# Eight raw buffers in turn for the expert weight blocks of a hybrid decoder step, three of them made of two half tiles from pools of the mixers

## Chip, cores and metric

One core of one Trainium2 chip runs one launch of the whole step. The metric is the device time of that launch in microseconds; less is better. The engines are named as in the profile: PE (TensorE, its weight loads PEld), ACT (ScalarE), DVE (VectorE), POOL (GpSimd) and SP (SyncE, which here only issues transfers).

## What is computed

The step runs two layers over 264 tokens (256 of a prompt, 8 decode tokens) of width 1024. Each layer mixes the tokens by three parallel groups (SSD, RWKV-7, GLA), projects, normalizes, and then has a channel mixer: a dense SwiGLU in layer 0, a top-2-of-8 mixture of experts in layer 1. The change touches the experts:

```python
def _moe(h, router, wg, wu, wd):
    logits = (h @ router).astype(jnp.float32)
    vals, idx = lax.top_k(logits, TOP_K)
    wts = jax.nn.softmax(vals, axis=-1)
    comb = jnp.sum(jax.nn.one_hot(idx, N_EXPERTS, dtype=jnp.float32) * wts[..., None], axis=-2).astype(h.dtype)
    out = jnp.zeros_like(h)
    for e in range(N_EXPERTS):
        out = out + comb[..., e:e + 1] * _swiglu(h, wg[e], wu[e], wd[e])
    return out
```

Each of `wg[e]`, `wu[e]`, `wd[e]` is 1024 x 1024 in f32.

## The kernel before

Every matrix product is made of three reduced-precision (fp32r) products: a weight block `w` is split into `wh`, its rounded copy, and `wl = w - wh`, and so are the activations; the product is xh·wh + xh·wl + xl·wh. A block is 128 x 1024 f32, 512 KB, and `block` (L380) does all of it: SP issues the transfer into a raw tile `w` (L384), ACT copies it to `wh` (through `act`, L296), DVE subtracts into `wl` (through `sub`, L317). The raw tile is free once both have read it; `wh` and `wl` are free once the block's last matmul has read them. `wh` and `wl` have three buffers each (`NW`, L253).

The experts' stage (`experts`, L1563) gathers each expert's tokens into 128 slots and runs the experts in four pairs. For one expert `up` (L1621) makes gate and up products in two halves of 512 columns, each half 2 x 4 blocks, then silu, product, four transposes and a split; `down` (L1644) makes the output in two halves of 4 blocks. That is 24 blocks an expert, 192 in all, used strictly in order. `expert_mm` (L1704) does a block: two k-slices, three matmuls of 512 columns each, in the order wh, wl, wh; so a block is six matmuls. After each block `pump` (L1613) may put in a step of gathering the next pair (tiles `xg`, `xo`, `sel`) or of scattering the previous one (`sc`).

Raw tiles come from two pools: `wts` (`self.wp`, three buffers, tag `w`) and `wada` (`self.ap`, two buffers, tag `wa`), the second otherwise used by the loads for the modulation (`ada`, L446, rows `wa<-in_wada`). The lambda `wl` at L1567 sends every block with an even number to `wada`, every odd one to `wts`:

```python
wl = lambda e, m, b: self.block(self.I["moe"][e, m, b], by="wmoe", spare=b % MOE["wa"] == 0)
```

Other tiles come from shared pools by a table (`T2`, L187): pool `g` has four buffers of 264 x 2 columns and serves, among others, `hk`, the four tiles that hold the experts' input; pool `m` has three and serves the decode states of the mixers (`srm` to `gsq`). `hk` is last read by the transposes `ht` (`rows`, L1517) at the head of the experts' stage.

Instructions are written in program order, and a scheduler orders them within each engine by priorities; tile reuse becomes semaphore waits. SP's queue runs in its order: a transfer that must wait for its buffer holds up all behind it. The last transfers before the stage are those of the output projection (`wout`, L637), the modulation (`wada`, L463) and the router (L1474).

Of the kernel before, what the change touches and what calls it, by code (L numbers as in the profile page):

```python
# [7 lines left out]
F32 = mybir.dt.float32  # L8
F32R = mybir.dt.float32r
# [157 lines left out]
def _unpack(r):  # L167
# [18 lines left out]

T2 = {'r': 'ai k r cs kk k2 ka rkt bk gn gr ah htl az',  # L187
 'd': 'hh hl cv qk gv zs xo bl xg al',
 'g': 'gqk gsc o hk sq rbt',
 'a': 'adae',  # L190
 'q': 'lw srw sss hts',
 'm': 'srm srv bx sst sgu sgl gsq'}
T1 = {'u': 'xt x ee fs raw', 'r': 'vt st vb q1 ab rt gt', 'd': 'xb', 't': 'w ends ed sm da dx rs8 mx cslot'}
TP = {'a': 'ada adat st',
 'd': 'pj op eg0 ed eg1 ssq pos lg',
# [3 lines left out]
ORDER = [['rwkv', 'conv', 'rstep', 'qkv', 'aff', 'sstep', 'rout', 'gstep', 'gla', 'ssd', 'z2', 'gread', 'z1', 'z0'],  # L199
 ['rstep', 'rwkv', 'conv', 'sstep', 'qkv', 'rout', 'gstep', 'aff', 'gla', 'ssd', 'z0', 'z1', 'z2', 'gread']]  # L200
X = {'FR': 1, 'AHEAD': 1, 'SA': 4}
MOE = {'s0': 28, 'ss': 6, 'g0': 31, 'gs': 5, 'wa': 2, 'e0': 11, 'es': 5}
LOW = {'rout.0': -9440,
 'win.1': -20,
 'sstep.0': -1560,
# [61 lines left out]
class Net:  # L267
    def __init__(self, nc, tc, I, O, stack):
        self.nc, self.tc, self.I, self.O = nc, tc, I, O
        p = lambda name, bufs, **k: stack.enter_context(tc.tile_pool(name=name, bufs=bufs, **k))  # L270
        self.cp = p("const", 1)
        self.wp = p("wts", NW["w"])
        self.ap = p("wada", NW["a"])
        self.hp = p("whi", NW["h"])
        self.lp = p("wlo", NW["l"])
        self.bp = p("big", 1)
        self.p2 = {t: p("f2" + t, n) for t, n in N2.items()}
        self.p1 = {t: p("f1" + t, n) for t, n in N1.items()}
        self.dp = p("scr", 1, space=bass.MemoryType.DRAM)
        self.pp = {t: p("ps" + t, n, space=PSUM) for t, n in NP.items()}  # L280
        self.late = None
        self.acts = []
        self.setname = None
        self.pre = None
        self.n = 0


    def act(self, out, in_, func=AF.Copy, bias=0.0, scale=1.0):
# [88 lines left out]
        return self.cst[:, o - 128:o - 128 + w]  # L377


    def block(self, src, n=1024, by="none", spare=False):  # L380

        self.n += 1
        w = (self.ap if spare else self.wp).tile([128, 1024], F32, tag="wa" if spare else "w", name=f"w_{self.n}")
        self.nc.sync.dma_start(w[:, :n], src)  # L384
        hi = self.hp.tile([128, 1024], F32R, tag="h", name=f"wh_{self.n}")
        lo = self.lp.tile([128, 1024], F32R, tag="l", name=f"wl_{self.n}")
        with self.low(by):
            self.act(hi[:, :n], w[:, :n])
            self.sub(lo[:, :n], w[:, :n], hi[:, :n].bitcast(F32))
        return hi[:, :n], lo[:, :n]  # L390
# [1172 lines left out]
    def experts(self, l, r, last, first=()):  # L1563

        nc, io = self.nc, self.C("iota")
        toks, mask, comb, pos, hth, htl = self.routed
        wl = lambda e, m, b: self.block(self.I["moe"][e, m, b], by="wmoe", spare=b % MOE["wa"] == 0)  # L1567
        if r:
            p = self.f1("posr", [128, 3, NE])
            self.ts(p, pos, -128.0 * r, OP.add)  # L1570
# [3 lines left out]
        def gather(pr):  # L1574

            sel = []
            for t, (t0, n) in enumerate(toks):
                s = self.f1("sel", [128, 2, 128], F32R)
                if t == 2:
                    nc.gpsimd.memset(s.bitcast(F32), 0.0)  # L1580
                for i in range(2):
                    e = 2 * pr + i
                    chosen = self.ts(s[:n, i], io[:n], pos[:n, t, e:e + 1], OP.is_equal, mask[:n, t, e:e + 1], OP.mult)
                sel.append(s)
            yield
            name = "xg" if pr % 2 else "xo"
            xg = [[self.f2(name, [128, 2, 256], F32R) for _ in range(4)] for _ in range(2)]
            for k in range(8):
                for x, src in zip(xg, (hth, htl)):
                    ps = self.ps("xg", [128, 256])  # L1590
                    for t, (t0, n) in enumerate(toks):
                        self.mm(ps, src[t, k // 4][:, k % 4], sel[t].rearrange("p a b -> p (a b)"), t == 0, t == 2)
                    done = self.act(x[k // 2][:, k % 2], ps)
                yield
            self.affine((chosen, done))
            pc = self.ps("cs", [128, 2])
            cslot = self.f1("cslot", [128, 2])
            selt = []
            for i in range(2):
                e = 2 * pr + i  # L1600
                for t, (t0, n) in enumerate(toks):
                    self.mm(pc[:, i:i + 1], sel[t][:n, i].bitcast(F32), comb[:n, t, e:e + 1], t == 0, t == 2)
                ps = self.ps("st")[:, :TT]
                for t, (t0, n) in enumerate(toks):
                    self.tr(ps[:, t0:t0 + n], sel[t][:n, i].bitcast(F32))
                s = self.f1("selt", [128, TT], F32R)
                self.act(s, ps)
                selt.append(s)
            self.act(cslot, pc)
            G[pr] = xg, selt, cslot  # L1610
            yield
# [43 lines left out]
        def scatter(pr):  # L1655
            selt = G[pr][1]
            if last and pr == 3:
                V["st"] = self.stats()
            st = V["st"]
            self.need(l, 5)  # L1660
            for d in range(8):
                ps = self.ps("sc")[:, :TT]
                todo = [(y[:, d % 4], selt[i]) for i, yh, yl in Y[pr, d // 4] for y in (yh, yl)]
                for j, (y, s) in enumerate(todo):
                    self.mm(ps, y, s, j == 0, j == 3)
                self.residual(l, 5, d, ps, st, last=st is not None)
                yield
# [8 lines left out]
        for pr in range(4):  # L1676
            ahead = gather(pr + 1) if pr < 3 else iter(())
            V["at"], V["side"] = 0, [(MOE["s0"], MOE["ss"], back), (MOE["g0"], MOE["gs"], ahead)]
            if pr < 3:
# [4 lines left out]
            else:  # L1684
                for i in range(2):
                    up(pr, i)
                for n in range(2):
                    for i in range(2):
                        down(pr, i, n)
                    if n == 0:  # L1690
                        for _ in back:
                            pass
                        back = scatter(pr)
                        V["side"] = [(V["at"] + MOE["e0"], MOE["es"], back)]
                break
# [8 lines left out]
    def expert_mm(self, ps, lhs, block, pump):  # L1704
        for q in range(4):
            hi, lo = block(q)
            for k in (2 * q, 2 * q + 1):
                xh, xl = lhs(k)
                w = slice(k % 2 * 512, k % 2 * 512 + 512)
                self.mm(ps, xh, hi[:, w], k == 0, False)  # L1710
                self.mm(ps, xh, lo[:, w], False, False)
                self.mm(ps, xl, hi[:, w], False, k == 7)
            pump()
# [25 lines left out]
```

## Time and profile before

| | us |
|---|---|
| median of 3 runs | 1132.21 |
| lowest and highest | 1125.35, 1136.5 |
| the profiled execution | 1124.54 |
| its span, first to last instruction | 1122.8 |
| PE busy in the span | 1023.5 (91%) |
| DVE busy | 741.4 (66%) |
| ACT busy | 609.1 (54%) |

The profile is of one execution, with a record of each instruction's start and duration and each transfer's landing. Matmuls are pipelined, so that PE counts as busy where they overlap; the step from one matmul's start to the next says more than its duration. Idle time is put down to what ended it. The mean granted TensorE clock was 0.96 of full speed, and 1.00 (2.4 GHz) throughout the experts' stage.

### The profile page before, as it was taken

The numbers are of one execution on the slowest core, as the hardware profiler recorded it, in microseconds if no ns is written. First come the engines' busy times: TensorE is split into PE (matmuls) and PEld (weight loads), VectorE is DVE, ScalarE is ACT, GpSimd is POOL, SyncE is SP. The second block draws the span as 40 slices with busy tenths as digits, with TensorE's granted clock in tenths as the row PEclk, the third lists the DMA queues.
The fourth block names the chain that finished last, engine by engine and source line by source line (L and its number), as shares of the span: only waits on it lengthen the run. The fifth ranks groups of instructions, "written<-read, shape, count | busy, mean of one in ns | idle before, by whom it ended". The sixth has DMA issues, their size and how long they took to land. (4 is left out here: it accounts for less than half of the span.)

```text
span 1122.8 us, 22443 instructions
## 1 busy us (share of the span) xinstructions
PE 1023.5 (91%) x8944; PEld 833.1 (74%) x8944; DVE 741.4 (66%) x1406; ACT 609.1 (54%) x1037; POOL 90.2 (8%) x191
## 2 busy tenths in 40 slices
PE   6889988789899999989899898979999999999994
PEld 2678766557799999978677775758777777778763
DVE  1577647654755545457786676476778888877884
ACT  2566323543554444348562445367767776776663
POOL 1031222000100000001411210010000000000000
PEclk9899989999899999999999989989999999999997
DMA  9774468754565555563863474316889988888881
GB/s 355 251 225 132 149 180 306 267 169 147 178 197 174 187 179 160 160 196 133 235 228 119 145 240 143 113 42 207 299 285 299 303 287 298 305 295 303 290 276 42
DMA packets 71184, 238.55 MB, mean 212 GB/s; under 512 B 9280, under 2 KB 10016, under 8 KB 71072
## 3 DMA queue, kind: packets, MB, share of 16 engines
q1 hardware_dynamic: 66512, 226.18, 61.1%
q0 software_dynamic: 4000, 10.71, 3.5%
q8 instruction: 72, 1.18, 0.4%
q14 instruction: 40, 0.33, 0.1%
q10 hardware_dynamic: 560, 0.15, 0.1%
HBM read 231.50 MB, written 5.51 MB: 211 GB/s over the span
## 5 line engine op out<-in xcount | busy, mean ns | idle before, releaser
L317 DVE TENSOR_TENSOR wl<-w,wh 128x1024 fp32r<-128x1024 f32 (+1 forms) x324 | 388.4, 1216 | 160.9 <-ACT wh L296 154.7
L296 ACT ACTIVATE wh<-w 128x1024 fp32r<-128x1024 f32 (+1 forms) x324 | 334.0, 1051 | 279.8 <-issue 79.5
L336 PE MATMUL pj<-hh,wh 128*128 128x264 f32 x384 | 122.1, 320 | 7.0 <-ACT cv L296 3.1
L336 PE MATMUL pj<-hl,wh 128*128 128x264 f32 x384 | 122.5, 320 | 0.4 <-DVE hl L317 0.4
L336 PE MATMUL pj<-hh,wl 128*128 128x264 f32 x384 | 120.6, 315 | 1.1 <-DVE wl L317 1.1
L336 PEld LDWEIGHTS pj<-hh,wh 128*128 128x128 f32 x384 | 80.0, 209 | 16.0 <-ACT hh L296 4.3
L336 PEld LDWEIGHTS pj<-hl,wh 128*128 128x128 f32 x384 | 79.7, 208 | 8.5 <-issue 6.0
L336 PEld LDWEIGHTS pj<-hh,wl 128*128 128x128 f32 x384 | 79.6, 208 | 7.6 <-issue 3.4
L336 PE MATMUL eg<-wh,xg 128*128 128x512 f32 x256 | 81.7, 397 | 0.5 <-ACT wh L296 0.5
L336 PE MATMUL eg<-wh,xo 128*128 128x512 f32 x256 | 81.7, 396 | 0.2 <-ACT wh L296 0.2
L336 PE MATMUL ada<-wa,sc 128*32 128x256 f32 x640 | 51.5, 404 | 27.0 <-DMA wa<-in_wada 23.2
L336 PE MATMUL ed<-wl,ath 128*128 128x512 f32 x128 | 52.9, 413 | 4.5 <-DVE wl L317 4.5
L336 PEld LDWEIGHTS eg<-wh,xg 128*128 128x128 f32 x256 | 48.1, 188 | 11.7 <-ACT wh L296 2.4
L336 PEld LDWEIGHTS eg<-wh,xo 128*128 128x128 f32 x256 | 48.1, 188 | 10.7 <-ACT wh L296 1.2
L336 PE MATMUL eg<-wl,xg 128*128 128x512 f32 x128 | 52.6, 411 | 3.8 <-DVE wl L317 3.6
L336 PE MATMUL eg<-wl,xo 128*128 128x512 f32 x128 | 52.6, 411 | 1.3 <-DVE wl L317 1.2
L336 PE MATMUL ed<-wh,ath 128*128 128x512 f32 x128 | 50.9, 397 | 0.4 <-ACT wh L296 0.3
L336 PE MATMUL fg<-hh,wh 128*128 128x264 f32 x176 | 50.8, 289 | 0.0
L336 PE MATMUL ed<-wh,atl 128*128 128x512 f32 x128 | 50.6, 395 | 0.0
L336 PE MATMUL fu<-hh,wh 128*128 128x264 f32 x176 | 50.5, 287 | 0.0
L336 PE MATMUL fu<-hh,wl 128*128 128x264 f32 x176 | 50.4, 286 | 0.0
L336 PE MATMUL fu<-hl,wh 128*128 128x264 f32 x176 | 50.4, 286 | 0.0
(486 smaller groups left out, 2288.7 us busy)
## 6 DMA issues: line engine op xcount, KB each, us to landing
w<-in_moe SPq DMA_DIRECT2D x192, 512.0 KB, 4.6
wa<-in_wada SPq DMA_DIRECT2D x80, 512.0 KB, 4.6
w<-in_win SPq DMA_DIRECT2D x48, 512.0 KB, 4.7
w<-in_ffgu SPq DMA_DIRECT2D x44, 512.0 KB, 3.7
k<-in_wada SPq DMA_DIRECT2D x32, 256.0 KB, 5.8
w<-in_wout SPq DMA_DIRECT2D x16, 512.0 KB, 4.9
w<-in_ffd SPq DMA_DIRECT2D x16, 512.0 KB, 3.5
w<-in_ffd SPq DMA_DIRECT2D x8, 384.0 KB, 3.9
```

The lines of the kernel that those rows point to most:

```text
L296: r = self.nc.scalar.activation(out, in_, func, bias=bias, scale=scale)
L317: return (e or self.nc.vector).tensor_tensor(out, a, b, op=op)
L336: return self.nc.tensor.matmul(out, lhsT, rhs, start=start, stop=stop)
```

## The change

The blocks of the experts' stage take their raw buffer from a string of eight letters in turn, `wawagwmg`: `w` is the pool `wts`, `a` is `wada`, `g` and `m` are two new names, `wg` and `wm`, in the mixers' pools `g` and `m`. A block of `g` or `m` is two tiles of 128 x 512 with a transfer, a conversion and a subtraction each. A counter runs over all blocks. No pool grows.

```diff
-  'g': 'gqk gsc o hk sq rbt',
+  'g': 'gqk gsc o hk sq rbt wg',
-  'm': 'srm srv bx sst sgu sgl gsq'}
+  'm': 'srm srv bx sst sgu sgl gsq wm'}
...
-MOE = {'s0': 28, 'ss': 6, 'g0': 31, 'gs': 5, 'wa': 2, 'e0': 11, 'es': 5}
+MOE = {'s0': 28, 'ss': 6, 'g0': 31, 'gs': 5, 'wa': 'wawagwmg', 'e0': 11, 'es': 5}
...
+        self.blocks = -1
...
-    def block(self, src, n=1024, by="none", spare=False):
+    def block(self, src, n=1024, by="none", home="w"):
 
         self.n += 1
+        if home not in "wa":
+            ws = [self.f2("wg" if home == "g" else "wm", [128, 512]) for _ in range(2)]
+            for i, w in enumerate(ws):
+                self.nc.sync.dma_start(w, src[:, i * 512:i * 512 + 512])
+            hi = self.hp.tile([128, 1024], F32R, tag="h", name=f"wh_{self.n}")
+            lo = self.lp.tile([128, 1024], F32R, tag="l", name=f"wl_{self.n}")
+            with self.low(by):
+                for i, w in enumerate(ws):
+                    cs = slice(i * 512, i * 512 + 512)
+                    self.act(hi[:, cs], w)
+                    self.sub(lo[:, cs], w, hi[:, cs].bitcast(F32))
+            return hi, lo
+        spare = home == "a"
...
-        wl = lambda e, m, b: self.block(self.I["moe"][e, m, b], by="wmoe", spare=b % MOE["wa"] == 0)
+        homes = MOE["wa"]
+
+        def wl(e, m, b):
+            self.blocks += 1
+            return self.block(self.I["moe"][e, m, b], by="wmoe", home=homes[self.blocks % len(homes)])
```

The order of instructions moves with it. The first number in a name counts the program's tiles. On SP, before, the queue ahead of the experts' stage is this; `w_1322` to `w_1325` are the expert blocks 0 to 3, `w_1327` to `w_1330` blocks 4 to 7, `w_1336` and `w_1337` blocks 8 and 9, and `w_1239`, `w_1243` the output projection's last two:

```order
L384 DMA w_1322_9294<-in_moe 128x1024
L384 DMA w_1324_9318<-in_moe 128x1024
L384 DMA w_1239_8911<-in_wout 128x1024
L384 DMA w_1243_8950<-in_wout 128x1024
L384 DMA w_1323_9306<-in_moe 128x1024
L384 DMA w_1325_9330<-in_moe 128x1024
L384 DMA w_1328_9355<-in_moe 128x1024
L384 DMA w_1327_9343<-in_moe 128x1024
L384 DMA w_1330_9379<-in_moe 128x1024
L384 DMA w_1329_9367<-in_moe 128x1024
L1474 DMA router_1256_9039<-in_router 128x256
L384 DMA w_1337_9417<-in_moe 128x1024
```

Of the change, the same place on SP, first part; `wm_1332` and `wm_1333` are the halves of block 6, `wm_1352` the first half of block 14, and blocks 0 to 3 have the names they had:

```order
L387 DMA wm_1332_9371<-in_moe 128x512
L387 DMA wm_1333_9372<-in_moe 128x512
L477 DMA wa_1235_8889<-in_wada 128x1024
L477 DMA wa_1236_8895<-in_wada 128x1024
L398 DMA w_1323_9306<-in_moe 128x1024
L398 DMA w_1325_9330<-in_moe 128x1024
L387 DMA wm_1352_9494<-in_moe 128x512
L398 DMA w_1239_8911<-in_wout 128x1024
L398 DMA w_1243_8950<-in_wout 128x1024
L398 DMA w_1322_9294<-in_moe 128x1024
L398 DMA w_1324_9318<-in_moe 128x1024
L398 DMA w_1330_9359<-in_moe 128x1024
```

Block 6 has moved ahead of two loads for the modulation, blocks 1 and 3 ahead of the output projection's last two, blocks 0 and 2 behind them; `w_1330` is now block 5. The queue goes on, around the router's load, with `w_1342` to `w_1344` blocks 8 to 10, `wg_1328` and `wg_1329` block 4, `wg_1335` and `wg_1336` block 7, `w_1345` block 11 and `wg_1348` block 12's first half:

```order
L398 DMA w_1342_9417<-in_moe 128x1024
L398 DMA w_1343_9429<-in_moe 128x1024
L398 DMA w_1344_9441<-in_moe 128x1024
L1488 DMA router_1256_9039<-in_router 128x256
L387 DMA wg_1328_9343<-in_moe 128x512
L387 DMA wg_1329_9344<-in_moe 128x512
L387 DMA wg_1335_9387<-in_moe 128x512
L387 DMA wg_1336_9388<-in_moe 128x512
L398 DMA w_1345_9453<-in_moe 128x1024
L387 DMA wg_1348_9466<-in_moe 128x512
```

Blocks 8 to 10 stand ahead of the router, where blocks 4 to 7 stood; blocks 4 and 7, in the tiles of `hk`, stand behind it. On DVE the subtractions at the head of the stage are these before, for blocks 3 to 8 (`w_1336` is block 8):

```order
L317 TENSOR_TENSOR wl_1325_9333<-w_1325_9330,wh_1325_9332 128x1024
L317 TENSOR_TENSOR wl_1327_9346<-w_1327_9343,wh_1327_9345 128x1024
L317 TENSOR_TENSOR wl_1328_9358<-w_1328_9355,wh_1328_9357 128x1024
L317 TENSOR_TENSOR wl_1329_9370<-w_1329_9367,wh_1329_9369 128x1024
L317 TENSOR_TENSOR wl_1330_9382<-w_1330_9379,wh_1330_9381 128x1024
L317 TENSOR_TENSOR wl_1336_9408<-w_1336_9405,wh_1336_9407 128x1024
```

and of the change, for blocks 3 to 6 and the first half of 7:

```order
L318 TENSOR_TENSOR wl_1325_9333<-w_1325_9330,wh_1325_9332 128x1024
L318 TENSOR_TENSOR wl_1329_9348<-wg_1328_9343,wh_1329_9347 128x512
L318 TENSOR_TENSOR wl_1329_9348<-wg_1329_9344,wh_1329_9347 128x512
L318 TENSOR_TENSOR wl_1330_9362<-w_1330_9359,wh_1330_9361 128x1024
L318 TENSOR_TENSOR wl_1333_9376<-wm_1332_9371,wh_1333_9375 128x512
L318 TENSOR_TENSOR wl_1333_9376<-wm_1333_9372,wh_1333_9375 128x512
L318 TENSOR_TENSOR wl_1336_9392<-wg_1335_9387,wh_1336_9391 128x512
```

The blocks keep their order on DVE (and on ACT); blocks of `g` and `m` have become two instructions of 512 columns.

## Rows read from the trace of the kernel before

**Rows 1.** Busy by stretch: start:end, length, PE, PEld, DVE, ACT, POOL, PEclk, DMA share, GB/s

```profile
14.00:28.00 14.00, 11.27 (x84) 4.61 (x84) 3.75 (x8) 4.45 (x7) 1.77 (x4) 1.00 1.05 400
28.00:42.00 14.00, 10.12 (x71) 7.23 (x72) 6.23 (x14) 6.36 (x10) 1.39 (x6) 0.88 0.78 284
...
678.00:708.00 30.00, 25.97 (x268) 19.50 (x270) 19.36 (x46) 14.38 (x34) 1.10 (x2) 0.94 0.35 125
...
765.00:1088.00 323.00, 312.36 (x1461) 247.89 (x1460) 259.34 (x313) 229.42 (x286) 0.62 (x2) 1.00 0.88 295
```

**Rows 2.** Waits, 760.6 to 1100.1 us: who waited for whom, us in total, times, longest

```profile
ACT wh L296 <- DMA w<-in_moe: 58.3, 63, 2.4
PEld eg L336 <- DVE wl L317: 11.5, 24, 1.1
PEld ed L336 <- DVE wl L317: 9.0, 17, 1.1
...
PEld eg L336 <- ACT wh L296: 3.6, 9, 0.7
...
PEld ed L336 <- ACT wh L296: 1.6, 3, 0.8
```

**Rows 3.** Timeline, one turn of a `wada` buffer: start, us, engine, instruction [idle before <-releaser]

```profile
795.23 0.33 SPq L384 DMA_DIRECT2D w<-in_moe  x1
...
799.62 1.06 ACT L296 ACTIVATE wh<-w 128x1024 fp32r<-128x1024 f32 x1 [0.80 <-DMA w<-in_moe]
...
800.71 1.23 DVE L317 TENSOR_TENSOR wl<-w,wh 128x1024 fp32r<-128x1024 f32 x1 [1.08 <-ACT wh L296]
...
801.97 0.33 SPq L384 DMA_DIRECT2D w<-in_moe  x1
```

**Rows 4.** The tensor `in_moe` after 765.2 us: its issues (duration ns, first, last), landing

```profile
L384 SPq DMA_DIRECT2D w<-in_moe x184: 327/328/792, 765.2 to 1088.6; - x184
...
DMA to landing us min/median/max: 3.6/4.7/6.8
```

**Rows 5.** Groups by form, 760 to 1100 us: count, busy us, mean ns, idle before <-releasers

```profile
L317 DVE TENSOR_TENSOR wl<-w,wh 128x1024 fp32r<-128x1024 f32 x189 | 225.5, 1222 | 65.1 <-ACT wh L296 60.1 <-PE eg L336 4.0 <-PE ed L336 0.5
L296 ACT ACTIVATE wh<-w 128x1024 fp32r<-128x1024 f32 x189 | 193.0, 1054 | 79.3 <-DMA w<-in_moe 58.3 <-DVE wl L317 6.8 <-DVE x L317 3.3
...
L336 PEld LDWEIGHTS eg<-wh,xg 128*128 128x128 f32 x256 | 48.1, 188 | 11.7 <-ACT wh L296 2.4
...
L317 DVE TENSOR_TENSOR atl<-eat,ath 128x512 fp32r<-128x512 f32 x16 | 10.9, 684 | 0.0
...
L296 ACT ACTIVATE ea<-eg 128x512 f32<-128x512 f32 x16 | 9.5, 594 | 3.6 <-PE eg L336 3.3
```

**Rows 6.** Timeline of PE, two expert matmuls that follow each other

```profile
886.44 0.40 PE L336 MATMUL ed<-wh,ath 128*128 128x512 f32 x1
886.67 0.40 PE L336 MATMUL ed<-wl,ath 128*128 128x512 f32 x1
```

**Rows 7.** Busy by stretch: from the first to past the last expert matmul

```profile
760.60:1100.10 339.50, 328.85 (x1546) 260.57 (x1546) 271.56 (x335) 241.60 (x306) 0.62 (x2) 1.00 0.85 285
```

**Rows 8.** The tile `sgl`: its readers `gso` on PE (duration ns, first and last start)

```profile
L336 PE MATMUL gso<-qk,sgl x64: 192/192/213, 683.7 to 685.4; 32*64 32x1 f32 x64
```

**Rows 9.** Timeline of SP and PE around the stage's start

```profile
687.62 0.33 SPq L463 DMA_DIRECT2D wa<-in_wada  x1
...
737.01 0.37 SPq L1474 DMA_DIRECT2D router<-in_router  x1
...
749.41 1.04 PE L369 MATMUL ht<-ident,hk 128*8 128x128 f32 x8
...
765.21 0.33 SPq L384 DMA_DIRECT2D w<-in_moe  x1
```

## The prediction

> **What bounds the kernel now.** I read the stretches first, then the waits, then single transfers. In the experts' stage (765 to 1088 us, 29% of the span) TensorE has work for 312.36 of 323 us at the full granted clock, and the transfer engines are busy 0.88 of the time at 295 GB/s [rows 1]: both look nearly full, so the shares alone decide nothing. The waits do. TensorE's weight loads stood 11.5 + 9.0 us for `wl` and 3.6 + 1.6 us for `wh`, 25.7 us at 24 + 17 + 9 + 3 = 53 places, and ScalarE, which makes `wh`, stood 58.3 us at 63 places for the landing of `w` [rows 2]. So TensorE waits for conversions, and these wait for transfers.
>
> Why are the transfers late, at 295 GB/s? The stretch 14 to 28 us moved 400 GB/s with the same 16 engines [rows 1]. They are late because they are asked for late. Even blocks live in the `wada` pool's two buffers, odd ones in `wts`'s three. An even block's transfer can't start before the even block four places earlier is converted. One turn of such a buffer can be read: the transfer was issued at 795.23; ScalarE started at 799.62, its 0.80 us of idle time ended by the landing; VectorE ran from 800.71 for 1.23 us; the next transfer was issued at 801.97 [rows 3]. That is 6.74 us for four blocks. From medians, a landing of 4.7 us, a conversion of 1.054 us, a subtraction of 1.222 us and some 0.1 us of hand-overs make 7.1 us, or 1.77 us a block [rows 3 to 5]. The stage's 184 transfers from 765.2 to 1088.6 us took 323.4 / 184 = 1.757 us each [rows 4]. The two-buffer loop explains the pace of the whole stage.
>
> What would TensorE do without it? Matmuls of 512 columns start 0.23 us apart [rows 6], six to a block, 192 blocks: 1152 x 0.232 = 267 us; the other matmuls fill the rest of the 339.5 us between 760.6 and 1100.1 [rows 7] that is not waiting, so the floor is 339.5 - 25.7 = 314 us, 1.63 us a block.
>
> **The change part by part.** *The ring.* Eight buffers in turn (3 `w`, 2 `wa`, 2 pairs `wg`, 1 and a half pairs `wm`) replace the split 2 + 3. Each block's transfer now waits for the block eight places earlier, so the 7.1 us loop spans eight blocks, 0.89 us a block, under TensorE's 1.63. What goes is the 25.7 us of waits. A little of it isn't loss: loads that follow each other without a wait also stand 0.232 - 0.188 = 0.044 us [rows 5], 53 x 0.044 = 2.3 us. Gain: 23.4 us.
>
> *What is late next.* `wh` and `wl` still have three buffers each. A conversion starts when TensorE leaves the block three places back and must be through before the second matmul of its own block: two blocks, 12 x 0.232 = 2.78 us, plus one matmul, 3.0 us in all; it needs 0.2 (ScalarE's start after a matmul, an estimate from the hand-overs in rows 3) + 1.05 + 0.03 + 1.22 + 0.05 = 2.55 us. The slack of some 0.45 us is eaten where ScalarE or VectorE has another operation of 0.59 to 0.75 us in front: the activation, transposed copy and output of each expert's half, 3 x 16 = 48 places. Each then costs about 0.68 - 0.45 = 0.23 us of TensorE, 11 us if all 48 meet a conversion and none if the transposes beside them give the time back. I take half, 6 us, and keep 0 and 12. For the low end speaks that 53 waits among 192 blocks are fewer than the 96 even ones: the odd blocks, whose data lie ready, go through the same ring of three today.
>
> *Halves.* Three of eight blocks, 72, are two transfers, two conversions and two subtractions of 512 columns. On VectorE 2 x 0.684 - 1.222 = 0.146 us more a block, 10.5 us; on ScalarE 2 x 0.594 - 1.054 = 0.134, 9.6 us [rows 5]. Both engines have room: VectorE's 271.56 us [rows 7] become 282 in some 322, 88%; ScalarE's 241.60 become 251, 78%. For such a block the first half is ready after 0.2 + 0.59 + 0.03 + 0.68 = 1.5 us rather than 2.55, so it has more slack, not less. Cost on the path: 0; if VectorE became the bound, up to 10.5 us, which the 12 us above already stand for. SP issues 264 transfers rather than 192, 0.33 us each [rows 3], 87 us of 320: no bound.
>
> *Ahead of the stage.* The new order puts the two halves of block 6 in front of two `wada` loads, the second half waiting for the mixers' last reader of its buffer. That reader, `gso` on TensorE, ends at 685.4 [rows 8]; the `wada` load behind it went out at 687.62 [rows 9]. Cover 2 us, cost 0; the transfer engines are busy 0.35 there [rows 1], so the extra 0.75 MB is carried for nothing. Blocks 8, 9 and 10 now stand ahead of the router's load, but they wait for the conversions of blocks 0, 1 and 2, the same three that blocks 4, 7 and 6 wait for now; the router still goes out at 737.0 [rows 9]. Blocks 4 and 7 use the tiles of `hk`, which are not dead yet: they wait for its last transposes, at 749.41 + 1.04 [rows 9], and everything behind them on SP waits too. Nothing there is wanted before 765: block 4 lands by about 755, and today SP stands from 737.0 to 765.21 anyway [rows 9]. When the stage starts, 11.5 blocks lie loaded instead of 8.
>
> *Sum.* The profiled execution took 1124.54 us (its span is 1122.8): 1124.5 - 23.4 + 6 = 1107.1 us. The median of the runs, 1132.21, is 7.7 us above it. A longer landing goes straight into the two-buffer loop: 0.1 us more is 46 turns x 0.1 = 4.6 us. If the runs differ by that, the change removes it; if by something else, it stays and the median is 1114.8. I take the middle, 1111 us.
>
> **One rule against the change.** The 256 KB halves fill the opening: 14 to 28 us, 400 GB/s [rows 1]. The Trainium skill (DMA: Bandwidth & Descriptors, Rules for kernel authors) wants transfers of 1 MiB or more for full bandwidth; by that rule cutting three of eight blocks in two is a step the wrong way, and the stage would stay bound by transfers. The trace disagrees as far as it goes: its best stretch is of halves. The sum keeps the row; the rule's case is the last rival.
>
> **The rivals.** *The conversions take over.* For: VectorE at 88% serves them in order, and the ring of three is short. Against: halves give slack, and odd blocks keep up today. At the 12 us bound and a bit more, 23.4 - 14 = 9 us are gained: 1115 on the profile's scale, 1119 to 1123 on the runs'. *The transfers are the bound already.* For: busy 0.88 at 295 GB/s. Against: the 400 GB/s, and SP waiting for buffers, not the engines. Then only the 3.5 blocks loaded ahead count, 3.5 x 1.757 = 6 us: 1118.5, or 1126 by the median. *No effect*, if `hk` or the order on SP held the prefetch so late that the early ring never fills: 1132. It would need SP to stand past 765, and what it waits for there is over at 750.5 [rows 9]. *Slower.* One mechanism: mixed whole and half transfers run less well than whole ones. After 765.2 180.5 blocks of 0.524 MB remain; under 180.5 x 0.524 / 323.4 = 292 GB/s the stage is longer than now. The stretch 28 to 42 us, a mix, shows 284 GB/s at a share of 0.78 [rows 1]; at that rate 180.5 x 1.846 = 333 us, 10 us more: 1134.5, or 1142 by the median.
>
> **How the numbers follow.** Forecast 0.74, with its own range 1100 to 1119; conversions 0.11; transfers 0.07; no effect 0.03; slower 0.05. 1% of 1132 is 11.3 us, about what a measurement of this kernel can tell from no change. The forecast gains 11 to 24 us and is faster by that but for its lowest part (0.03); of the conversions' case a third is. Faster 0.75, within 1% 0.21, slower 0.04 (the fifth of the slower case that stays within 1% goes there). The range 1100 to 1125 reaches through the conversions' case and leaves out the two beyond it and a little below.
>
> **What would show it.** Right: ScalarE's waits for the landing of expert blocks fall from 58.3 us to under 10, the weight loads' waits for `wl` from 20.5 us to about 6, and what is left is preceded by a late start of VectorE or ScalarE, not by a landing; transfers are issued 10 us or more before their conversion; the stage from the first to the last expert matmul is about 322 us. Wrong: conversions that still wait for landings at 300 GB/s (transfers), or VectorE busy throughout with TensorE waiting as long as before (conversions), or `wada`, `router` or `hk` reached later than 687.6, 737.0 and 750.5 us.

## The result, and the profile after

| | before | after |
|---|---|---|
| median of 4 runs of each, side by side on one chip | 1128.78 us | 1109.58 us |
| lowest and highest | 1123.45, 1136.5 | 1106.2, 1112.74 |
| the profiled execution | 1124.54 | 1112.09 |
| its span | 1122.8 | 1110.2 |
| first expert matmul starts at | 760.67 | 762.98 |
| the stage: to the end of the last expert matmul | 337.83 | 319.26 |
| the end: from there to the end of the span | 24.25 | 27.97 |

The ratio is 0.9856, with a 95% interval of 0.9809 to 0.9904: 11 to 22 us shorter. The last three rows of the table are read from the first and last record of the tiles `eg` and `ed` on TensorE; they add up to the span. The stage lost 18.6 us, the end gained 3.7, and the first expert matmul came 2.3 us later. Medians in this document are of all executions of a kernel, while ratios and intervals leave out the slow ones, more than 1.5% above that kernel's fastest.

Busy time by stretch of the kernel after, the four stretches of [rows 1] and one around the stage, as [rows 7] (start:end, length, PE, PEld, DVE, ACT, POOL, granted clock, DMA share, GB/s):

```profile
14.00:28.00 14.00, 11.39 (x84) 4.82 (x84) 3.75 (x7) 4.45 (x7) 1.77 (x4) 0.89 1.05 400
28.00:42.00 14.00, 10.32 (x68) 7.81 (x69) 6.62 (x15) 6.36 (x10) 1.39 (x6) 0.76 0.77 286
678.00:708.00 30.00, 26.05 (x258) 18.79 (x258) 18.51 (x45) 13.00 (x30) 1.10 (x2) 0.89 0.45 137
765.00:1088.00 323.00, 319.77 (x1536) 260.65 (x1534) 277.06 (x408) 250.83 (x374) 0.62 (x2) 1.00 0.83 294
762.90:1082.50 319.60, 316.37 (x1516) 259.42 (x1516) 274.10 (x394) 250.34 (x374) 0.62 (x2) 1.00 0.84 297
```

The reader is to see how little the shares tell: from 765 to 1088 us the transfer engines carry 294 GB/s, as before (295), at a lower share, and TensorE's busy time rises by 7 us. From 678 to 708 us the half transfers of blocks 6 and 14 in pool `m` are added (137 GB/s instead of 125).

The waits of the kernel after, 760.6 to 1100.1 us, against [rows 2] (who waited for whom, us, times, longest):

```profile
ACT wh L297 <- PE eg L337: 32.2, 99, 1.3
...
ACT wh L297 <- PE ed L337: 7.0, 22, 0.7
...
PEld ed L337 <- ACT ea L297: 2.0, 5, 0.5
...
PEld xg L337 <- ACT xg L297: 1.3, 4, 0.7
PEld xg L337 <- ACT xo L297: 1.1, 3, 0.7
...
PEld eg L337 <- DVE wl L318: 0.4, 2, 0.2
```

ScalarE's 58.3 us for landings are gone from the list. What it waits for now is TensorE, 39.2 us at 121 places, to free a buffer of the ring of three `wh`. Of the weight loads' 20.5 us for `wl`, 0.4 is left, in two waits. The line and the engine have turned round: conversions no longer make TensorE late, TensorE paces them. New in the list are waits of the weight loads for other results of ScalarE, the activation `ea` and the gathered inputs `xg` and `xo`, of which the list before has none.

The transfers after 765.2 us, against [rows 4], from the view of the tensor `in_moe`, and SP's queue in a piece of the stage:

```profile
L398 SPq DMA_DIRECT2D w<-in_moe x112: 327/328/755, 767.5 to 1066.6; - x112
...
DMA to landing us min/median/max: 3.2/5.0/7.3
```

```profile
816.42 1.04 SPq L387 DMA_DIRECT2D wg<-in_moe  x2
```

```profile
826.14 1.15 ACT L297 ACTIVATE wh<-wg 128x512 fp32r<-128x512 f32 x2 [0.28 <-PE ed L337]
```

The two transfers issued at 816.42 are converted at 826.14, 9.7 us later, and the 0.28 us of idle time ahead of that conversion is ended by TensorE, where [rows 3] had a landing. Over the records of the `wg` tiles issue and conversion lie 10.2 us apart (median), the landing 6.2 us before the conversion. A landing takes 5.0 us (whole and half transfers together) instead of 4.7, and ScalarE never waits for one.

### The profile page after: what moved, and what is told of

Read it like the earlier page. It is cut to its first block, busy times and chain, and to the rows that moved or that the text cites. A ratio compares the mean times of both kernels' runs of the same rounds, so it can differ in the third digit from the quotient of the medians.

```text
span 1110.2 us, 22791 instructions
## 1 busy us (share of the span) xinstructions
PE 1019.3 (92%) x8944; PEld 834.0 (75%) x8944; DVE 747.0 (67%) x1478; ACT 620.1 (56%) x1109; POOL 87.3 (8%) x191
## 5 line engine op out<-in xcount | busy, mean ns | idle before, releaser
L297 ACT ACTIVATE wh<-w 128x1024 fp32r<-128x1024 f32 (+1 forms) x252 | 264.8, 1052 | 222.4 <-issue 79.4
L318 DVE TENSOR_TENSOR wl<-w,wh 128x1024 fp32r<-128x1024 f32 (+1 forms) x252 | 304.7, 1215 | 124.5 <-ACT wh L297 121.4
L337 PE MATMUL pj<-hh,wl 128*128 128x264 f32 x384 | 118.1, 309 | 1.1 <-DVE wl L318 1.1
L337 PEld LDWEIGHTS pj<-hh,wh 128*128 128x128 f32 x384 | 77.3, 202 | 15.7 <-ACT hh L297 4.3
L337 PEld LDWEIGHTS pj<-hl,wh 128*128 128x128 f32 x384 | 77.0, 201 | 8.6 <-issue 6.2
L337 PEld LDWEIGHTS pj<-hh,wl 128*128 128x128 f32 x384 | 77.0, 201 | 8.0 <-issue 3.8
L318 DVE TENSOR_TENSOR wl<-wg,wh 128x512 fp32r<-128x512 f32 x96 | 61.9, 687 | 0.5
L297 ACT ACTIVATE wh<-wg 128x512 fp32r<-128x512 f32 x96 | 55.1, 623 | 6.6 <-PE eg L337 5.0
L337 PE MATMUL eg<-wl,xg 128*128 128x512 f32 x128 | 50.5, 395 | 0.0
L337 PE MATMUL fg<-hh,wl 128*128 128x264 f32 x176 | 50.5, 287 | 0.0
L337 PE MATMUL ed<-wl,ath 128*128 128x512 f32 x128 | 50.4, 394 | 0.0
```

What stands on the lines that cost most here:

```text
L297: r = self.nc.scalar.activation(out, in_, func, bias=bias, scale=scale)
L318: return (e or self.nc.vector).tensor_tensor(out, a, b, op=op)
L337: return self.nc.tensor.matmul(out, lhsT, rhs, start=start, stop=stop)
```

## The experiments

For every kernel the table gives the same readings of its profiled execution. The last two columns are a sum over the stage: for each matmul the time to the start of the next, less the median of its tile and shape, where that is over 20 ns; first where the next is an expert matmul (`eg`, `ed`), then where it is another one (gather `xg`, scatter `sc`, and the like). Each row is read from one trace.

| kernel | median us | first expert matmul | stage | end | stage + end | lost at `eg`, `ed` | at others |
|---|---|---|---|---|---|---|---|
| before | 1128.78 | 760.67 | 337.83 | 24.25 | 362.1 | 25.4 | 2.5 |
| after | 1109.58 | 762.98 | 319.26 | 27.97 | 347.2 | 5.7 | 5.6 |
| after, again | 1107.39 | 752.48 | 319.31 | 28.19 | 347.5 | 5.7 | 5.6 |
| turn `wawaw` | 1101.17 | 756.25 | 319.11 | 23.60 | 342.7 | 8.0 | 1.8 |
| turn `wawaw`, again | 1103.84 | 756.93 | 319.46 | 23.48 | 342.9 | 8.2 | 1.8 |
| turn `awagawam` | 1129.12 | 765.01 | 340.09 | 25.55 | 365.6 | 27.7 | 3.9 |
| turn `aaw` | 1209.91 | 757.16 | 426.39 | 24.25 | 450.6 | 99.6 | 13.6 |
| halves only, old turn | 1120.89 | 763.64 | 332.89 | 25.43 | 358.3 | 20.1 | 3.3 |
| all conversions in halves | 1112.10 | 767.55 | 320.00 | 27.86 | 347.9 | 3.9 | 8.0 |
| turn `wawawg` | 1108.19 | 758.11 | 317.15 | 27.68 | 344.8 | 6.1 | 3.1 |
| after, early scatter | 1107.57 | 770.54 | 323.07 | 24.82 | 347.9 | 6.3 | 5.9 |
| turn `wawaw`, early scatter | 1103.07 | 759.12 | 321.74 | 22.54 | 344.3 | 7.5 | 2.5 |

**A fair turn of the five old buffers.** The first question was whether the distance between two uses of a `wada` buffer set the pace (theory T1), or whether the room and the blocks loaded ahead did (T2).

```diff
-MOE = {'s0': 28, 'ss': 6, 'g0': 31, 'gs': 5, 'wa': 'wawagwmg', 'e0': 11, 'es': 5}
+MOE = {'s0': 28, 'ss': 6, 'g0': 31, 'gs': 5, 'wa': 'wawaw', 'e0': 11, 'es': 5}
```

> Only the five buffers of before (3 w, 2 wada), but in the fair turn w a w a w: no tile of the mixers, no halves, every transfer waits for the block five places earlier instead of four (wada) or six (wts). Theory T1, the distance of four set the pace: the 7.1 us loop spans five blocks, 1.42 us a block, under TensorE's 1.66 (319.3 us / 192 in the changed kernel); a landing of 6.8 us, the 90th percentile before, makes the loop 9.2 us or 1.84 a block, so some landings are still waited for. Stage from the first to the last expert matmul 322 to 328 us, ScalarE's waits for expert blocks under 20 us, time 1110 to 1118 us. Rival T2, more room and more blocks loaded ahead bring the gain: with five buffers the stage stays near 338 us and the time at 1125 to 1132 us.

1101.17 us (1100.29 to 1102.01), ratio 0.9766 to before (0.9721 to 0.9810). T1 holds, and T2 falls: without one tile of the mixers and without a half, the stage is as short as that of the changed kernel. Stage and time are even below what T1 expected. It had taken 6.8 us for the 90th percentile of the landings before; that is the longest of [rows 4], and the 90th percentile in the trace is 5.3 us, with which the loop over five blocks stays under TensorE's 1.66. The waits, 740 to 1110 us:

```profile
ACT wh L297 <- DMA w<-in_moe: 11.3, 22, 1.2
...
PEld eg L337 <- DVE wl L318: 3.7, 10, 1.1
PEld ed L337 <- DVE wl L318: 2.4, 6, 0.7
```

Five buffers are just enough: 50 of the 192 blocks landed less than 0.2 us before their conversion starts (the median is 0.6 us), and 22 are waited for, 40 in the second trace of this kernel. The changed kernel, with 6.2 us of margin at its `wg` blocks, loses 2.3 us less at the expert matmuls (5.7 instead of 8.0).

**Eight buffers, the even blocks still at four.**

```diff
-MOE = {'s0': 28, 'ss': 6, 'g0': 31, 'gs': 5, 'wa': 'wawagwmg', 'e0': 11, 'es': 5}
+MOE = {'s0': 28, 'ss': 6, 'g0': 31, 'gs': 5, 'wa': 'awagawam', 'e0': 11, 'es': 5}
```

> All eight buffers, but the turn is a w a g a w a m: the even blocks stay in the two wada buffers at a distance of four blocks as before, the odd ones go through w, g, w, m. T1: the loop of four blocks is still 7.1 us, so the pace stays at 1.75 us a block, the stage at 334 to 340 us and the time at 1124 to 1132 us, though six tiles' worth of room is added. T2: room and prefetch count, the stage is near 320 us and the time 1108 to 1114 us.

1129.12 us, ratio 1.0017 (0.9986 to 1.0047): no gain from three more buffers, and a stage of 340.09 us, at the top of what T1 expected. Its waits in the stage are those of [rows 2] again:

```profile
ACT wh L297 <- DMA w<-in_moe: 51.0, 56, 2.5
PEld eg L337 <- DVE wl L318: 13.2, 24, 1.1
PEld eg L337 <- ACT wh L297: 7.9, 17, 1.0
PEld ed L337 <- DVE wl L318: 6.9, 14, 1.1
```

The `wg` blocks of this kernel lay loaded for 22 us (median) before they were converted, but TensorE takes the blocks in order, and the `wada` block beside them was late.

**A distance of three.**

```diff
-MOE = {'s0': 28, 'ss': 6, 'g0': 31, 'gs': 5, 'wa': 'wawagwmg', 'e0': 11, 'es': 5}
+MOE = {'s0': 28, 'ss': 6, 'g0': 31, 'gs': 5, 'wa': 'aaw', 'e0': 11, 'es': 5}
```

> The five buffers of before in the turn a a w: a wada buffer comes back after three blocks. T1: 7.1 us / 3 = 2.37 us a block at the landing of before (4.7 us), 2.0 at the shortest tenth of landings (3.6 us); 192 blocks make a stage of 384 to 455 us and a time of 1175 to 1246 us; ScalarE waits for two of three landings. T2 (the number of buffers decides, whatever the turn): as with five buffers in the other turn.

1209.91 us, ratio 1.0729 (1.0668 to 1.0790): five buffers in another turn are far slower, as T1 said, and T2 falls again. The stage of 426.39 us is 2.22 us a block, times three a loop of 6.66 us. Before, 337.83 / 192 x 4 = 7.04; in the kernel `awagawam` 340.09 / 192 x 4 = 7.09. The loop is the same within the landing time, which is 4.4 us here and 4.7 there:

```profile
L398 SPq DMA_DIRECT2D w<-in_moe x181: 327/328/604, 768.0 to 1172.7; - x181
...
  ACT wh L297: 126.9, 92
...
DMA to landing us min/median/max: 3.4/4.4/5.8
```

ScalarE waits for 92 landings, not for two of three (128). (The 3.6 us that the expectation calls the shortest tenth is the shortest landing of [rows 4]; a tenth is under 4.2 us.)

With a distance of five the same loop would allow 1.4 us a block, and TensorE, which takes 1.66, sets the pace. That is the law of this stage in the turns measured: the pace is the larger of TensorE's time for a block and the loop over the distance.

**Halves alone.** The buffers and turn of before, every conversion in halves.

```diff
-            self.act(hi[:, :n], w[:, :n])
-            self.sub(lo[:, :n], w[:, :n], hi[:, :n].bitcast(F32))
+            for cs in ((slice(0, 512), slice(512, 1024)) if by == "wmoe" else (slice(0, n),)):
+                self.act(hi[:, cs], w[:, cs])
+                self.sub(lo[:, cs], w[:, cs], hi[:, cs].bitcast(F32))
...
-MOE = {'s0': 28, 'ss': 6, 'g0': 31, 'gs': 5, 'wa': 'wawagwmg', 'e0': 11, 'es': 5}
+MOE = {'s0': 28, 'ss': 6, 'g0': 31, 'gs': 5, 'wa': 'aw', 'e0': 11, 'es': 5}
```

> The buffers and the turn of before (even blocks in wada, odd in wts, distances four and six), and only the conversions of every expert block cut into halves of 512 columns; transfers whole. T1: the loop of a wada buffer becomes landing 4.65 + start 0.1 + ScalarE's half 0.61 + 0.05 + VectorE's two halves 2 x 0.687 + issue 0.1 = 6.9 us instead of 7.1 (the second half of ScalarE runs beside VectorE), 1.72 us a block: stage 328 to 336 us, time 1116 to 1126 us. Rival T3, the shorter chain from landing to the first matmul (about 1 us less for a first half) is what helped the changed kernel: the stage is near 320 us and the time near 1108 us.

1120.89 us, ratio 0.998 (0.9946 to 1.0014). The stage is 332.89 us, 6.94 us for four blocks against 6.9 reckoned: only what the halves cut from the loop is won. Landings are still waited for, here from 740 to 1110 us:

```profile
ACT wh L297 <- DMA w<-in_moe: 45.0, 48, 2.0
PEld eg L337 <- ACT wh L297: 9.4, 18, 1.1
```

So the shorter chain isn't what helped the changed kernel.

**All conversions in halves**, on top of the changed kernel: the same edit of the conversion, with the turn `wawagwmg` kept.

> The changed kernel, with the whole blocks of the experts (five of eight) also converted in two halves of 512 columns, as the blocks in g and m are; transfers stay whole. Price by the rows: 120 blocks x 0.146 = 17.5 us more on VectorE (260.65 of the 323 us from 765 to 1088 in the changed kernel become 278, 87%) and 16 us on ScalarE. Theory A, TensorE is the bound of the stage now and conversions have slack: stage 319 us within 2, time within 3 us of the changed kernel's 1109.6. Theory B, conversions against the rings of three wh and wl still cost (the 6 us of the prediction): the first half is ready about 1 us earlier, TensorE's spacing beyond its medians falls from 11.3 us to about 6, and the time is 4 to 6 us shorter. Theory C, VectorE is nearly the bound: 6 to 17 us longer, with TensorE waiting for wl.

1112.1 us (1103.88 to 1117.21), ratio 0.9846 (0.9805 to 0.9887). Stage + end is 347.9 us against 347.2 and 347.5 of the changed kernel: theory A. The expectation itself took VectorE's time from the wrong column (260.65 is the weight loads'; VectorE had 277.06). In its stage the kernel shows

```profile
767.50:1087.60 320.10, 316.97 (x1515) 259.76 (x1515) 283.81 (x511) 260.56 (x491) 0.62 (x2) 1.00 0.84 297
```

VectorE rises by 9.7 us over the changed kernel's 274.10, not 17.5. The margin of a block's whole `wl` before its second matmul, from the records, is 0.84 us (median) instead of 0.51; that of the first half, which is all that this matmul reads, 1.45 instead of 0.81. It wins 1.8 us at the expert matmuls and loses 2.4 at the others: theory B's gain is there and is eaten.

**Fewer halves.** Six buffers, one block of six in halves.

```diff
-MOE = {'s0': 28, 'ss': 6, 'g0': 31, 'gs': 5, 'wa': 'wawagwmg', 'e0': 11, 'es': 5}
+MOE = {'s0': 28, 'ss': 6, 'g0': 31, 'gs': 5, 'wa': 'wawawg', 'e0': 11, 'es': 5}
```

> Six buffers in the turn w a w a w g: the distance is six, and one block of six is in halves (32 of 192, not 72). If halves cost by their number (TensorE's spacing beyond its medians at gathers, scatters and transposes of the stage: 1.8 us without halves, 5.6 with 72, 8.0 with all 192), this has 2.5 to 3.5 us there, and less than the 8 us at expert matmuls that the turn w a w a w has; the stage is 317 to 319 us. The order of TensorE has 29 scatter matmuls behind the last expert matmul, so the end is 27 to 28 us: stage and end 345 to 347 us, between the changed kernel's 347.3 and the 342.8 of w a w a w; time 1102 to 1112 us. Rival: the more buffers, the better; stage and end under 342 us.

1108.19 us, ratio 0.9874 (0.9824 to 0.9923); stage 317.15, end 27.68, together 344.8, a hair under the range expected. What is lost at matmuls other than the experts' goes, in the kernels that TensorE paces, with the number of blocks in halves: 1.8 us with none, 3.1 with 32, 5.6 with 72, 8.0 with 192. This kernel's stage is the shortest of all, and its end the changed kernel's.

**The changed kernel and the five buffers once more, on one chip.**

> The changed kernel as it is, once more, beside the next three on one chip. Theory P: what differs between runs of one kernel lies ahead of the experts' stage and in the granted clock there, not in the landing times of the stage. In eight traces so far the same instructions reach the first expert matmul between 756.3 and 767.6 us, while the stage of the changed kernel took 319.3 us. So here the first expert matmul comes anywhere from 756 to 768 us, the stage takes 318 to 321 us and the end 27.5 to 28.5 us; time 1104 to 1114 us. Rival (the prediction's): the spread comes from landings; then the stage differs by several us from 319.3 when the time does.

> The five buffers in the turn w a w a w once more, on one chip with the changed kernel. Stage 319 us and end 23.6 us again; against the changed kernel on this chip 4 us shorter, all of it from the end (16 scatter matmuls behind the last expert matmul, not 32), since the 8 to 9 us between the medians of the first runs hold 4 to 5 us of the stretch ahead of the stage, where both have the same instructions in the same order. Rival: the three more buffers cost ahead of the stage as well (their 11.5 blocks are loaded from 677 us on); then this is 8 us shorter again and its first expert matmul comes earlier by 4 us or more.

1107.39 us (1101.86 to 1110.43) and 1103.84 us (1101.59 to 1111.85). Both have the stage and end that they had. In the trace the five buffers are 4.6 us shorter there (347.5 less 342.9), all of it in the end; the intervals of their ratios to before, 0.9798 to 0.9893 and 0.9777 to 0.9880, overlap, so by times alone it isn't settled. The rival of the second expectation falls: its first expert matmul came more than 4 us later than the changed kernel's, not earlier.

What differs between runs is elsewhere. The changed kernel's two profiled executions took 1112.09 and 1101.86 us; this is its first matmul `op` in each, and the stretch ahead of it:

```profile
L337 PE MATMUL op<-yh,wh x128: 278/283/479, 250.7 to 734.7; 128*128 128x264 f32 x128
...
60.00:250.00 190.00, 167.58 (x2334) 125.32 (x2335) 117.56 (x302) 78.28 (x180) 30.90 (x56) 0.91 0.65 206
```

and the second of them:

```profile
L337 PE MATMUL op<-yh,wh x128: 278/284/480, 241.6 to 724.3; 128*128 128x264 f32 x128
...
60.00:250.00 190.00, 165.95 (x2396) 126.23 (x2397) 122.62 (x314) 82.99 (x189) 30.91 (x56) 0.96 0.67 211
```

9.1 of the 10.2 us are there by 250 us, in the same instructions of the same program, and the granted clock beside them is 0.91 and 0.96. Followed matmul by matmul, most of it arises in one stretch: the 623 matmuls that start from 205.00 to 262.07 us in the first run start from 204.04 to 251.45 us in the second. The first of these views is of the first run, the other of the second:

```profile
205.00:265.00 60.00, 52.11 (x640) 35.02 (x639) 31.75 (x77) 26.85 (x64) 1.67 (x3) 0.86 0.55 179
```

```profile
205.00:255.00 50.00, 44.27 (x637) 30.42 (x637) 30.56 (x76) 26.73 (x64) 1.67 (x3) 1.00 0.63 211
```

In the stage the clock is 1.00 in both and the stages agree to 0.1 us. Theory P holds, but for its lower bound: the first expert matmul came at 752.48 us, 3.5 us before the earliest expected. Why the clock fell in one run and not in the other isn't shown.

**The end.** In the kernel after, TensorE's order has 32 scatter matmuls behind the last expert matmul. The tile `sc` there, in the kernel after, before, and with the five buffers:

```profile
L337 PE MATMUL sc<-selt,eyh x16: 282/286/392, 1082.1 to 1092.3; 128*128 128x264 f32 x16
L337 PE MATMUL sc<-selt,eyl x16: 281/284/392, 1082.2 to 1092.4; 128*128 128x264 f32 x16
```

```profile
L336 PE MATMUL sc<-selt,eyh x8: 278/286/392, 1099.5 to 1103.4; 128*128 128x264 f32 x8
L336 PE MATMUL sc<-selt,eyl x8: 281/286/392, 1099.7 to 1104.2; 128*128 128x264 f32 x8
```

```profile
L337 PE MATMUL sc<-selt,eyh x8: 282/284/389, 1076.3 to 1080.3; 128*128 128x264 f32 x8
L337 PE MATMUL sc<-selt,eyl x8: 281/287/388, 1076.5 to 1081.1; 128*128 128x264 f32 x8
```

The last scatter matmul starts 10.5 us after the last expert matmul (1081.85) in the kernel after and 6.1 us in the other two. This order is the scheduler's: in the kernel after it puts the first half of the last pair's scatter, which before stood among the expert matmuls, behind them. Why isn't shown. Behind the last expert matmul stand 16 scatter matmuls before and with `wawaw`, 12 with `aaw`, 20 with halves only in the old turn, 21 with `awagawam`, 29 with `wawawg`, 31 with all conversions in halves and 32 in the kernel after; that goes neither with the number of halves (20 with all 192 blocks in halves, 29 with 32) nor with that of the buffers. The end goes with it: 23.5 to 24.3 us with 12 to 16, 25.4 and 25.6 with 20 and 21, 27.7 to 28.2 with 29 to 32. Two kernels pull it forward, the changed one and, with the same edit, the five buffers:

```diff
-MOE = {'s0': 28, 'ss': 6, 'g0': 31, 'gs': 5, 'wa': 'wawagwmg', 'e0': 11, 'es': 5}
+MOE = {'s0': 28, 'ss': 6, 'g0': 31, 'gs': 5, 'wa': 'wawagwmg', 'e0': 1, 'es': 2}
```

> The changed kernel with the first steps of the last pair's scatter called from the 1st of the last eight blocks on, every 2nd block, instead of after them. TensorE's order then has 20 scatter matmuls behind the last expert matmul instead of 32 (16 in the kernel before). Theory Q: the 3.7 us that the changed kernel gave back at the end (27.97 us after the last expert matmul instead of 24.25) are the 16 scatter matmuls, their sums on VectorE and the squares and statistics hung on them, all in a chain there and hidden in the stage before. Then the end shrinks to 24 to 25.5 us and the stage grows by their TensorE time, 12 x 0.12 = 1.5 us: net 1 to 3 us shorter than the kernel without it. Rival: the end has its own bound (statistics and the final norm) and stays near 28 us; time the same or 1.5 us longer.

> The turn w a w a w and the early scatter together: 14 scatter matmuls behind the last expert matmul. End 22.5 to 23.6 us, stage 319 us: 0 to 1 us shorter than with the turn alone; the best of the four. If the end has its own bound, no difference.

The ends shrink as expected, to 24.82 and 22.54 us. The stages grow by 3.8 and 2.3 to 2.6 us, more than expected, since 8 to 9 statistics matmuls `ms`, 0.25 us each, come along with the scatters. Stage + end is 347.9 (before the edit 347.2 to 347.5) and 344.3 (342.7 to 342.9): nothing won in the trace. The medians are 1107.57 and 1103.07 us. The six runs of the first spread from 1098.91 to 1120.28 us; its ratio, 0.9817 (0.9759 to 0.9874), lies 0.003 below that of the changed kernel on the same chip and well inside its interval, so the times don't settle the 1 to 3 us expected. The profiled execution of the first of these was long ahead of the stage (first expert matmul at 770.5 us, granted clock 0.88 from 60 to 250 us); in its stage the clock is 1.00, as in the others. So most of what the end shows is work that has changed places. That the five buffers have the scatters in the stage at no cost there, while the forced order pays for them, wasn't taken further.

The shortest stage and end, 342.7 and 342.9 us, are those of the turn `wawaw` with the five buffers of before; in the program of the kernel after it is a change of one string. Its medians are 1101.17 and 1103.84 us; by times, the same turn with the early scatter (1103.07) isn't told from it.

## Why the prediction was right, point by point

**The bound, and the pace by the two-buffer loop: right, and shown.** 7.1 us over a distance of four was reckoned from medians; distances of three and four measured 6.66, 7.04 and 7.09, halves alone 6.94. At distances of six and eight TensorE sets the pace, and at five nearly so.

**The gain of 23.4 us: 19.7 measured.** What is lost at expert matmuls fell from 25.4 to 5.7 us. The forecast had 23.4 and gave 6 back. It put the gain down to the ring of eight; five buffers in a fair turn have 17.4 of these us (25.4 to 8.0), so most of the gain is the turn's and not the room's.

**The conversions' 6 us: the right size for the wrong cause.** The weight loads' waits for `wl` and `wh` are 0.4 us in all, not 6. The slack that the step reckoned, 0.45 us, is there (0.46 at the lower quartile, 0.51 at the median of 192 blocks); it was the 48 places that don't cost: only 14 blocks came within 0.1 us. That is the low end kept in the step; that the transposes and gathers give the time back, as it supposed, isn't shown. Of the 5.7 us that are left, 2.3 stand at six matmuls whose weight loads wait for `ea`, and 3.3 are 34 gaps of about 0.1 us for which the trace names nobody. So where the step had ScalarE's other operations delaying conversions, the trace has it the other way round: those operations come late for TensorE. The changed kernel also loses 3.1 us more than before at gathers and scatters (2.5 to 5.6), and its weight loads there wait 3.5 us for ScalarE's `xg` and `xo`, at nine places, where before they waited for neither. This loss goes with the halves, as shown above; that the conversions ahead of `xg`, `xo` and `ea` in ScalarE's order make them late is the likely cause, but no run moved them. The halves were costed at nothing on the path; they go with about 3 us.

**The halves' busy time: ScalarE right by two errors that cancel, VectorE too high.** Against the five buffers, whose stage is as long and shows

```profile
756.20:1075.40 319.20, 317.45 (x1532) 259.10 (x1535) 271.40 (x334) 241.47 (x304) 0.63 (x2) 1.00 0.87 303
```

the changed kernel has 2.7 us more on VectorE and 8.9 on ScalarE; the step said 10.5 and 9.6. The means of one half, 687 and 623 ns, were predicted as 684 and 594. But two halves that follow each other overlap on VectorE:

```profile
796.25 1.28 DVE L318 TENSOR_TENSOR wl<-wm,wh 128x512 fp32r<-128x512 f32 x2
...
798.65 1.22 DVE L318 TENSOR_TENSOR wl<-w,wh 128x1024 fp32r<-128x1024 f32 x1
```

1.28 us for a pair, not 2 x 0.687 = 1.37, against 1.22 for a whole block. On ScalarE a pair takes 1.15 us from first start to last end, not 2 x 0.623 = 1.25: the half was longer than predicted and the overlap made up for it. The 2.7 us on VectorE are also less by what left the stage with the scatters; the kernel with all conversions in halves has 9.7 us more for 120 blocks, 0.08 a block, which is 5.8 us for 72.

**Ahead of the stage, at nothing: right.** SP around the stage's start, in the kernel after, against [rows 9]:

```profile
737.99 0.37 SPq L1488 DMA_DIRECT2D router<-in_router  x1
750.99 1.77 SPq L387 DMA_DIRECT2D wg<-in_moe  x4
```

The `wada` load behind the second half of block 6 goes out at 687.16, 2.5 us after the last `gso` ends, as it does in kernels that put nothing into pool `m` (2.1 to 3.0). The router goes out 3.02 us after the last `op` matmul starts, in both kernels; the halves for `hk`'s tiles go out at 750.99, when its transposes are through. The 2.3 us by which the stage starts later lie where the profiled runs differ anyway: 752 to 771 us over twelve executions. From the last `gso` to the last `op` the kernel after takes 50.5 us where the trace before took 48.6; but the kernels without blocks in `m` take 50.1 to 50.5 too, so the halves in front of the `wada` loads aren't what makes it longer.

**The end: missed.** No step looked at where the scheduler would put the last pair's scatter. It cost 3.7 us at the end, of which 16 x 0.12 = 1.9 us are TensorE time that left the stage; so much of the stage's 18.6 us is work that moved, and stage and end together won 14.9 us. (The medians of the stage's matmuls add up to 309.7 us instead of 312.6; the rest of these 2.9 us is 1 to 2 ns less at each expert matmul.)

**The scale: wrong, and hidden by the middle.** The step that put the runs' spread down to landing times failed: executions 10.2 us apart had the same stage. The sum on the profile's own scale was 1107.1 us, and the profiled execution took 1112.1: 5 us worse than the steps, 4 of them the end and 2.3 the start of that run, less 1 in the stage. Had the median been carried over whole, the forecast would have been 1114.8; with the middle it was 1111, and 1109.58 was measured. That this is so near is in part luck. The median before came down from 1132.21 to 1128.78 us with the fourth run, and the medians lie 19.2 us apart where the steps had 17.4 and stage and end won 14.9; the rest lies ahead of the stage, where runs of one kernel differ by more.

**The rule on large transfers.** The Trainium skill (DMA: Bandwidth & Descriptors, Rules for kernel authors) asks for 1 MiB or more a transfer for full bandwidth. Here the kernel with 144 transfers of 256 KB carries 297 GB/s through its stage and the kernel with none 303, at stages of the same length. In neither are the transfers the bound, so no run here shows what halves would cost at the limit.

**The rivals.** Conversions as the bound, and transfers: ruled out by the waits above. No effect by a prefetch held too late: SP's last transfers ahead of the stage are out by 752.8 us, and ScalarE waits for no landing in the stage. (The kernel `awagawam` reaches no effect another way: the buffers are there and the turn isn't fair.) Slower by mixed transfers: the stage needs no more than the 294 GB/s it had, and one slice of the profile's page in it reaches 362.

## What to carry to other kernels

A pool of buffers paces a stream by its loop (issue, landing, conversion, release) over the number of blocks between two uses of the same buffer, and the worst pool paces all, since the blocks are used in order. Read one turn in the timeline, divide by the distance, compare with the consumer's time for a block; where one pool's distance is short, deal the buffers out fairly before looking for more. Where a scheduler orders the program, look also at what it does to the last instructions: the edit here won 18.6 us in the stage and lost 3.7 at the end to an order that nobody had touched, half of it work that had only moved.

## What the runs showed of the hardware

Twelve executions, with all but the same order on TensorE ahead of the stage, reach the first expert matmul between 752.5 and 770.5 us. The clock granted from 60 to 250 us goes with it, if not strictly: 0.96 in the runs that are there at 752.5 and 756.3, 0.95 in the four from 756.9 to 760.7, 0.91 or 0.92 in the three from 763.0 to 767.6, 0.88 at 770.5 (and 0.93 at 759.1, 0.94 at 763.6). At this size, differences of 5 us between kernels are read from the stretch that the change touches, not from the total time.

Two tensor operations of 512 columns that follow each other on VectorE take 1.28 us together where each is recorded with 0.687. On ScalarE two of 0.623 take 1.15.
